# Four seven-product pairs in the V chunk of a hybrid encoder layer, and the sums of x spread over other steps

## The chip, the cores and the metric

The kernel runs on one core of one Trainium2 chip. The metric is the device time of one execution in microseconds (us); of several runs the median is taken. Engines are named as the profile names them: PE (TensorE), DVE (VectorE), ACT (ScalarE), POOL (GpSimd) and SP, whose queue issues the loads.

## What is computed

One layer over 256 tokens of width 4096, all in float32. With its shapes, cut to what matters here:

```python
h = layer_norm(x, emb_ln_g, emb_ln_b)                # 256 x 4096
p = h @ w_in                                         # 4096 -> 13312 columns: conv B, C, h, z; q, k, v; attention gate
y_conv = c_b * centred_short_conv(c_c * c_h, conv_w) * silu(c_z)
y_attn = banded_window_attention(a_q, a_k, a_v, sink) * silu(a_z)
y = concatenate([y_conv, y_attn], -1) @ w_out        # 4096 x 4096
out = layer_norm(DN_ALPHA * h + y, ln_g, ln_b)
```

## The kernel before

**Chunks and pieces.** The columns of `w_in` are worked off in 26 chunks of 512 columns, in the order `IN_ORDER`: K, then V, then four times an attention gate (AZ) and a Q chunk, then the convolution's chunks. A chunk has 32 row tiles of 128 (`kt`). A plain piece holds four of them (128x2048, 1 MB). Each weight piece is split into a high half, which ACT rounds (`split_hi`, L197), and a low half, which DVE gets by a subtraction (`split_lo`, L201). PE then makes three products for each tile of weights: high by high, high by low, low by high (`mm`, L238 to L240). A plain step has 4 x 2 x 3 = 24 matmuls of 512 columns.

**Pairs.** In most chunks some row tiles are worked off two at a time with Strassen's seven products instead of eight (`mm_pair`, L244). A pair is one step of 7 x 3 = 21 matmuls of 256 columns. Its weights come as four blocks of 128x256 (`ws`, 0.5 MB); three more blocks are sums of them, made on DVE by three additions (`sums`, L178 to L180); ACT and DVE then split seven blocks (128x1792). The sums of x that a pair multiplies lie in the tile `SC`. `x_sums` (L609) makes them once for each of six pairs: five additions on DVE into the tile `xs` (L613, L618), then two copies on ACT (L480) and two subtractions on DVE (L481) that write `SC` and one quarter of `xT`. The second half of the even row tile's x in `xT` is overwritten there, so no plain step may use that row tile later. At a chunk's end the partial sums in `pacc` are put together: one copy on ACT (`pair_copy`, L642), four additions on DVE (`pair_sums`, L649 to L652), and two additions of `acc` (`whole`, L657).

**Steps.** A chunk's order is a string: `s` is a plain piece and `S` a pair. Before the change the K and V chunks have eight plain steps each (steps 0 to 7 and 8 to 15), and every chunk from AZ on has `sSsSSsSsSSs`, eleven steps. The first seven steps are written out in the prologue with the first LayerNorm; from step 7 on one loop issues everything, and each engine's queue has the order of this loop:

```python
mm_pair(j) if kind == "pair" else mm(j)
split_hi(j + 3)
for fn, a in later.pop(j, []):
    fn(*a)
...
loads(j)
sums(j + 4)
split_lo(j + 3)
```

So the high half and the low half of step j + 3 are issued at step j, and the sums of a pair one step earlier. `split_hi(j + 3)` writes one of three buffers and so waits for the matmuls of step j. The loads go through four weight buffers in these chunks; a load waits until the step that had the buffer has its low half.

**The chunk ends that matter here.** `end_k` (L487) copies the two accumulators of K to SBUF on ACT at step 7 (L490). `k_turn` (L492), at step 8, transposes them on PE (L476), right behind the matmuls of step 8, and splits the result (L480, L481). `end_v` (L496) splits the two accumulators of V at step 15 directly from PSUM. The mask table `tab` (L458 to L466) is made on DVE just ahead of step 7's work; its first operation waits for POOL.

Of the kernel before, what the change touches and what calls it, by code (L numbers as in the profile page):

```python
# [8 lines left out]
F32 = mybir.dt.float32  # L9
# [5 lines left out]
P = 128  # L15
D = 4096
S = 256
# [17 lines left out]
NPC = KT // PK  # L35
IN_ORDER = [C_K, C_V]
# [4 lines left out]
HW = W // 2  # L41
HT = S // 2
NP = 6
PAIRS = [0, 0] + [NP] * (len(IN_ORDER) - 2)
ORDERS = {0: "s" * 8, NP: "sSsSSsSsSSs"}
OUT = 100
OP = 4
OUT_ORDERS = ["s" * 8] * 2 + ["sSsSsSsSss"] * 4 + ["s" * 8, "", ""]
# [3 lines left out]
def units(ci):  # L52

    q, p, us = 2 * PAIRS[ci] // PK, 0, []
    for u in ORDERS[PAIRS[ci]]:
        if u == "s":
            us.append(("in", ci, q))
            q += 1
        else:
            us.append(("pair", ci, p))  # L60
            p += 1
    assert q == NPC and p == PAIRS[ci]
    return us
# [18 lines left out]
def npairs(ci):  # L82
    return PAIRS[ci] if ci < OUT else OUT_ORDERS[ci - OUT].count("S")

# [10 lines left out]
def encoder_kernel(ctx: ExitStack, tc: tile.TileContext, x, emb_g, emb_b, wi, ws, conv_w, sink, wo, ln_g, ln_b, out):  # L95
# [59 lines left out]
    def loads(j):  # L155

        nonlocal nxt
        while nxt < len(steps) and nxt <= j + 7:
            (u, _), bs = w_bufs(nxt)
            if u > j + (2 if len(bs) > N_W else 3):  # L160
                break
            load(nxt)
            nxt += 1
# [31 lines left out]
    def split_hi(j):  # L195
        wh[j] = half_tile(j, "whi")
        nc.scalar.activation(part(j, wh[j]), part(j, raw[j]), AF.Copy)  # L197

    def split_lo(j):
        wl[j] = half_tile(j, "wlo")  # L200
        nc.vector.tensor_tensor(part(j, wl[j]), part(j, raw[j]), part(j, wh[j]).bitcast(F32), op=ALU.subtract)  # L201
        raw.pop(j)
# [20 lines left out]
    acc = {}  # L223

    def mm(j):
        _, ci, q = steps[j]
        hi, lo = wh.pop(j), wl.pop(j)
        first = j == 0 or steps[j - 1][1] != ci
        last = j == N_IN - 1 or steps[j + 1][1] != ci
        for k in range(PK):  # L230
            kt = q * PK + k
            for i in range(2):
                if first and k == 0:
                    acc[ci, i] = ps_acc.tile([P, W], F32, name="acc")
                a = acc[ci, i]
                xh, xl = xT[:, kt, i * P:(i + 1) * P], xT[:, kt, S + i * P:S + (i + 1) * P]
                hk, lk = hi[:, k * W:(k + 1) * W], lo[:, k * W:(k + 1) * W]
                nc.tensor.matmul(a, xh, hk, start=(first and k == 0), stop=False)  # L238
                nc.tensor.matmul(a, xh, lk, start=False, stop=False)  # L239
                nc.tensor.matmul(a, xl, hk, start=False, stop=(last and k == PK - 1))  # L240
# [3 lines left out]
    def mm_pair(j):  # L244


        _, ci, p = steps[j]
        hi, lo = (t.pop(j).rearrange("p (b w) -> p b w", w=HW) for t in (wh, wl))
        last = p == npairs(ci) - 1
        if p == 0:  # L250
            for k in range(2):
                pacc[ci, k] = ps_p.tile([P, 2, HW], F32, name="pacc")
        a, b = 2 * p, 2 * p + 1
        x = lambda kt, i: (xT[:, kt, i * HT:(i + 1) * HT], xT[:, kt, (2 + i) * HT:(3 + i) * HT])
        sc = lambda n: (SC[:, p, 0, n, :], SC[:, p, 1, n, :])
        p0, p1, c0, c1 = pacc[ci, 0], pacc[ci, 1], acc[ci, 0], acc[ci, 1]
        for (ah, al), w, o, opens, closes in (
                (x(a, 0), 2, p0[:, 0, :], True, False), (x(b, 0), 3, c0[:, 0:HW], False, False),
                (sc(2), 1, c0[:, HW:W], False, False), (x(b, 1), 7, c1[:, 0:HW], False, False),
                (sc(0), 5, p1[:, 1, :], True, False), (x(a, 1) if ci < OUT else sc(3), 6, p0[:, 1, :], False, True),  # L260
                (sc(1), 4, p1[:, 0, :], False, True)):
            nc.tensor.matmul(o, ah, hi[:, w, :], start=(opens and p == 0), stop=False)  # L262
            nc.tensor.matmul(o, ah, lo[:, w, :], start=False, stop=False)  # L263
            nc.tensor.matmul(o, al, hi[:, w, :], start=False, stop=(closes and last))  # L264
# [13 lines left out]
    with tc.tile_pool(name="pro", bufs=1) as pro:  # L278
        warm = small.tile([P, 1], F32, name="sd", bufs=1)
        nc.scalar.activation(warm, eps_t, AF.Abs_reciprocal_sqrt)  # L280
        xs = [pro.tile([P, D], F32, name=f"x{i}") for i in range(2)]
# [171 lines left out]
    pa = ph.enter_context(tc.tile_pool(name="pa", bufs=1))  # L453
# [4 lines left out]
    def build_tab():  # L458
        ti = pa.tile([P, 2, S], F32, name="ti", tag="s")
        nc.gpsimd.iota(ti, pattern=[[-P, 2], [1, S]], base=0, channel_multiplier=-1,  # L460
                       allow_small_or_imprecise_dtypes=True)
        tf = pa.tile([P, 2, S], F32, name="tf", tag="p", bufs=2)
        nc.vector.tensor_scalar(tf, ti, -1.0, None, op0=ALU.mult)
        nc.vector.tensor_tensor(tf, tf, ti, op=ALU.max)
        nc.vector.tensor_scalar(ti, tf, float(WINDOW), NEG, op0=ALU.is_gt, op1=ALU.mult)
        nc.vector.tensor_tensor(tab, ti, tf, op=ALU.subtract)  # L466
# [12 lines left out]
    def halves(hi, lo, src):  # L479
        nc.scalar.activation(hi, src, AF.Copy)  # L480
        nc.vector.tensor_tensor(lo, src, hi.bitcast(F32), op=ALU.subtract)  # L481
# [3 lines left out]
    v = pa.tile([P, 2, 2, W], F32R, name="v")  # L485
# [8 lines left out]
            halves(kT[:, 2 * b:2 * b + 2, 0, :], kT[:, 2 * b:2 * b + 2, 1, :], ps)  # L494

    def end_v(ci, g):  # L496
        for i in range(2):
            halves(v[:, i, 0, :], v[:, i, 1, :], acc.pop((ci, i)))

    def end_z(ci, g):  # L500
        st_["z"] = whole(ci)
# [107 lines left out]
    def x_sums(p, t):  # L609

        x = xT[:, 2 * p:2 * p + 2, :]
        xf = t[:, 0:2 * S].rearrange("p (k t) -> p k t", k=2)
        nc.vector.tensor_tensor(xf, x[:, :, 0:S].bitcast(F32), x[:, :, S:2 * S].bitcast(F32), op=ALU.add)  # L613
        a11, a12, a21, a22 = (xf[:, k, i * HT:(i + 1) * HT] for i in range(2) for k in range(2))
        s = t[:, 2 * S:4 * S].rearrange("p (k t) -> p k t", k=4)
        for k, o0, o1, op in ((0, a21, a22, ALU.subtract), (3, s[:, 0, :], a11, ALU.subtract),
                              (1, a11, a21, ALU.subtract), (2, a12, s[:, 3, :], ALU.add)):
            nc.vector.tensor_tensor(s[:, k, :], o0, o1, op=op)  # L618
        if SC.shape[3] == 4:
            return halves(SC[:, p, 0, :, :], SC[:, p, 1, :, :], s)  # L620
        halves(SC[:, p, 0, :, :], SC[:, p, 1, :, :], s[:, 0:3, :])
        halves(x[:, 0, HT:2 * HT], x[:, 0, 3 * HT:4 * HT], s[:, 3, :])
# [17 lines left out]
    def pair_copy(ci):  # L640
        e = st_["e", ci] = sum_tile(ci)
        nc.scalar.activation(e[:, 0, 0:HW], pacc[ci, 0][:, 0, :], AF.Copy)  # L642
# [11 lines left out]
    def whole(ci):  # L654
        t = st_.pop(("e", ci))
        for i in range(2):
            nc.vector.tensor_tensor(t[:, i, :], acc.pop((ci, i)), t[:, i, :], op=ALU.add)  # L657
        return t
# [60 lines left out]
    def y_lo(q):  # L719
        for hi, lo, y in y_parts(q):  # L720
            nc.vector.tensor_tensor(lo, y, hi.bitcast(F32), op=ALU.subtract)

    build_tab()
    later = {}

    def at(j, fn, *a):
        later.setdefault(j, []).append((fn, a))

    ENDS = [(C_AZ, end_z), (C_V, end_v), (C_K, end_k), (C_Q, end_q), (C_CZ, end_cz), (C_CH, end_ch), (C_CC, end_cc),
            (C_CB, end_cb)]  # L730

# [28 lines left out]
    nxt = n_pro + 6  # L760
    last0 = N_IN - len(ORDERS[PAIRS[-1]])
    for t, f, q in ((3, y_load, 0), (5, y_hi, 0), (6, y_lo, 0), (6, y_load, 1), (7, y_hi, 1), (8, y_lo, 1), (8, y_load, 2),
# [5 lines left out]
    for j in range(n_pro, N_IN):  # L768
        kind, ci, q = steps[j]
        if j == z0 - 18:  # L770
            extra.clear()
        if j == z0 + 6:
            extra.insert(0, (pw, "w6"))
# [4 lines that stand above are left out]
        if kind == "pair" and q == PAIRS[ci] - 1:  # L778
            pair_copy(ci)
            at(j + 1, pair_sums, ci)  # L780
        if ci == 1 and 2 <= q < 2 + NP:
            x_sums(q - 2, pa.tile([P, 4 * S], F32, name="xs", tag="zT"))
        if steps[j + 1][1] != ci or j == N_IN - 1:
            if ci == c_ch0:
                at(j + 4, open_pc)
            if PAIRS[ci]:
                at(j + 1, chunk_end, j + 1, ci)
            else:
                chunk_end(j, ci)
# [3 lines that stand above are left out]
# [176 lines left out]
    for n, (c0, w, pk, j0) in enumerate(chunks):  # L969
        us = out_units(n)  # L970
        np_ = sum(u[0] == "opair" for u in us)
        for t, (kind, _, q) in enumerate(us):
            j = j0 + t
# [117 lines left out]
```

## Time and profile before

| what | value |
|---|---|
| median of 3 runs | 1543.43 us (1542.38 to 1543.45) |
| the profiled execution, its own time | 1543.44 us |
| span of the profile (first to last instruction) | 1541.7 us |
| PE busy | 1525.8 us, 99% of the span |
| DVE busy | 1271.7 us, 82% |
| ACT busy | 756.1 us, 49% |
| granted clock | 1.000 |

All times in the trace count from the span's start. In a timeline a row is: start, duration, engine, line, operation, output and inputs, shape, count, and in brackets the idle time before it and what ended it. A PE row's duration overlaps the next matmul; how long a matmul takes in a row of them is read from the distance between two starts. An engine's duration overlaps a little with the next start too, so what an operation costs a busy queue is the distance from its start to the next one's. In a list of waits a row gives the total, the number of times and the longest.

### The profile page before, as it was taken

The numbers are of one execution on the slowest core, as the hardware profiler recorded it, in microseconds if no ns is written. First come the engines' busy times: TensorE is split into PE (matmuls) and PEld (weight loads), VectorE is DVE, ScalarE is ACT, GpSimd is POOL, SyncE is SP. The second block draws the span as 40 slices with busy tenths as digits, with TensorE's granted clock in tenths as the row PEclk, the third lists the DMA queues.
The fourth block names the chain that finished last, engine by engine and source line by source line (L and its number), as shares of the span: only waits on it lengthen the run. The fifth ranks groups of instructions, "written<-read, shape, count | busy, mean of one in ns | idle before, by whom it ended". The sixth has DMA issues, their size and how long they took to land.

```text
span 1541.7 us, 21128 instructions
## 1 busy us (share of the span) xinstructions
PE 1525.8 (99%) x8654; PEld 1325.1 (86%) x8654; DVE 1271.7 (82%) x1441; ACT 756.1 (49%) x640; POOL 1.3 (0%) x7
## 2 busy tenths in 40 slices
PE   7999999999999999999999999999999999999998
PEld 4888888888888888888888888888888888888897
DVE  7778798888897888898888889888888688888656
ACT  4545556556465554544544445444455444444331
POOL 0000000000000000000000000000000000000000
PEclk9999999999999999999999999999999999999999
DMA  7635554545545456656555655556557756666753
GB/s 283 223 138 203 205 191 169 196 175 182 203 158 188 164 188 238 217 191 208 194 199 191 219 205 186 187 208 218 192 188 274 276 185 225 253 203 235 252 182 140
DMA packets 67392, 313.51 MB, mean 203 GB/s; under 512 B 8064, under 2 KB 12128, under 8 KB 43488
## 3 DMA queue, kind: packets, MB, share of 16 engines
q1 hardware_dynamic: 66288, 310.33, 56.5%
q10 hardware_dynamic: 1008, 1.84, 0.3%
q8 instruction: 68, 1.11, 0.3%
q14 instruction: 28, 0.23, 0.0%
HBM read 304.19 MB, written 7.86 MB: 202 GB/s over the span
## 4 chain that ended last, share of the span: by engine, by line
PE 93%; DVE 3%; issue 2%; ACT 2%; DMA 0%; SPq 0%; ACTq 0%
PE acc L238 15%; PE acc L240 15%; PE acc L239 15%; PE acc L879 7%; PE acc L881 7%; PE acc L880 7%; PE pacc L263 5%; PE pacc L262 5%; PE pacc L264 4%; PE acc L263 3%; PE acc L262 3%; PE acc L264 3%; DVE wlo L201 1%; ACT whi L197 1%; PE att L476 1%
## 5 line engine op out<-in xcount | busy, mean ns | idle before, releaser
L197 ACT ACTIVATE whi<-w 128x2048 fp32r<-128x2048 f32 (+1 forms) x330 | 600.0, 1818 | 671.1 <-PE acc L240 292.3
L201 DVE TENSOR_TENSOR wlo<-w,whi 128x2048 fp32r<-128x2048 f32 (+1 forms) x330 | 712.1, 2164 | 200.1 <-ACT whi L197 198.3
L238 PE MATMUL acc<-whi,xT 128*128 128x512 f32 x1072 | 424.5, 396 | 0.0
L240 PE MATMUL acc<-whi,xT 128*128 128x512 f32 x1072 | 420.1, 392 | 0.0
L239 PE MATMUL acc<-wlo,xT 128*128 128x512 f32 x1072 | 417.4, 389 | 0.7 <-DVE wlo L201 0.7
L240 PEld LDWEIGHTS acc<-whi,xT 128*128 128x128 f32 x1072 | 201.3, 188 | 47.0
L239 PEld LDWEIGHTS acc<-wlo,xT 128*128 128x128 f32 x1072 | 201.3, 188 | 41.6 <-DVE wlo L201 1.0
L238 PEld LDWEIGHTS acc<-whi,xT 128*128 128x128 f32 x1072 | 201.5, 188 | 37.5
L879 PE MATMUL acc<-whi,xT 128*128 128x512 f32 (+1 forms) x496 | 182.9, 369 | 0.0
L881 PE MATMUL acc<-whi,xT 128*128 128x512 f32 (+1 forms) x496 | 181.8, 366 | 0.0
L880 PE MATMUL acc<-wlo,xT 128*128 128x512 f32 (+1 forms) x496 | 180.5, 364 | 0.0
L178 DVE TENSOR_TENSOR w<-w 128x512 f32<-128x512 f32 x154 | 105.2, 683 | 4.5 <-DMA w<-in_ws 4.5
L881 PEld LDWEIGHTS acc<-whi,xT 128*128 128x128 f32 x496 | 93.0, 188 | 16.9
L880 PEld LDWEIGHTS acc<-wlo,xT 128*128 128x128 f32 x496 | 93.1, 188 | 15.5
L879 PEld LDWEIGHTS acc<-whi,xT 128*128 128x128 f32 x496 | 93.2, 188 | 14.2 <-issue 0.4
L263 PE MATMUL acc<-wlo,xT 128*128 128x256 f32 x320 | 89.4, 279 | 0.0
L262 PE MATMUL acc<-whi,xT 128*128 128x256 f32 x320 | 89.3, 279 | 0.0
L264 PE MATMUL acc<-whi,xT 128*128 128x256 f32 x320 | 89.1, 279 | 0.0
L262 PE MATMUL pacc<-whi,xT 128*128 128x256 f32 x304 | 86.9, 286 | 0.0
L263 PE MATMUL pacc<-wlo,xT 128*128 128x256 f32 x304 | 84.9, 279 | 0.0
L264 PE MATMUL pacc<-whi,xT 128*128 128x256 f32 x304 | 84.7, 279 | 0.0
L263 PE MATMUL pacc<-wlo,SC 128*128 128x256 f32 x288 | 81.0, 281 | 0.0
(230 smaller groups left out, 1873.8 us busy)
## 6 DMA issues: line engine op xcount, KB each, us to landing
w<-in_wi SPq DMA_DIRECT2D x134, 1024.0 KB
w<-in_ws SPq DMA_DIRECT2D x154, 512.0 KB
w<-in_wo SPq DMA_DIRECT2D x43, 1024.0 KB
R<-in_wo SPq DMA_DIRECT2D x13, 1024.0 KB
x<-in_x SPq DMA_DIRECT2D x7, 512.0 KB
yl<-yd SPq DMA_DIRECT2D x7, 512.0 KB
xc<-in_x SPq DMA_DIRECT2D x14, 256.0 KB
R<-in_ws SPq DMA_DIRECT2D x6, 512.0 KB
```

What stands on the lines that cost most here:

```text
L178: nc.vector.tensor_tensor(s01, b22, b12.to_broadcast([P, 2, HW]), op=ALU.add)
L197: nc.scalar.activation(part(j, wh[j]), part(j, raw[j]), AF.Copy)
L201: nc.vector.tensor_tensor(part(j, wl[j]), part(j, raw[j]), part(j, wh[j]).bitcast(F32), op=ALU.subtract)
L238: nc.tensor.matmul(a, xh, hk, start=(first and k == 0), stop=False)
L239: nc.tensor.matmul(a, xh, lk, start=False, stop=False)
L240: nc.tensor.matmul(a, xl, hk, start=False, stop=(last and k == PK - 1))
L262: nc.tensor.matmul(o, ah, hi[:, w, :], start=(opens and p == 0), stop=False)
L263: nc.tensor.matmul(o, ah, lo[:, w, :], start=False, stop=False)
L264: nc.tensor.matmul(o, al, hi[:, w, :], start=False, stop=(closes and last))
L879: nc.tensor.matmul(o, yh, hk, start=first, stop=False)
L880: nc.tensor.matmul(o, yh, lk, start=False, stop=False)
L881: nc.tensor.matmul(o, yl, hk, start=False, stop=last)
```

## The change

The V chunk gets four pairs. Its order is `sssSSsSsSs`: six plain steps and four pairs, steps 8 to 17, instead of eight plain steps. All later chunks keep their order and stand two steps later in the count. Since V now has partial sums in `pacc`, its end is the one that pair chunks have, one step late: `pair_copy` at step 16, `pair_sums` at 17, and at 18 `end_v`, which first calls `whole` and then splits the sum from SBUF.

`x_sums`, before at steps 10 to 15, is now called at the steps in `X_SUMS`: 7, 8, 10, 12, 14 and 16. Pairs 0 to 3 are first used at steps 11, 12, 14 and 16, and pairs 4 and 5 in the AZ chunk.

```diff
-PAIRS = [0, 0] + [NP] * (len(IN_ORDER) - 2)
-ORDERS = {0: "s" * 8, NP: "sSsSSsSsSSs"}
+VP = 4
+PAIRS = [0, VP] + [NP] * (len(IN_ORDER) - 2)
+ORDERS = {0: "s" * 8, VP: "sssSSsSsSs", NP: "sSsSSsSsSSs"}
...
     def end_v(ci, g):
+        t = whole(ci)
         for i in range(2):
-            halves(v[:, i, 0, :], v[:, i, 1, :], acc.pop((ci, i)))
+            halves(v[:, i, 0, :], v[:, i, 1, :], t[:, i, :])
...
+    X_SUMS = [NPC + k for k in (-1, 0, 2, 4, 6, 8)]
...
-        if ci == 1 and 2 <= q < 2 + NP:
-            x_sums(q - 2, pa.tile([P, 4 * S], F32, name="xs", tag="zT"))
+        if j in X_SUMS:
+            x_sums(X_SUMS.index(j), pa.tile([P, 4 * S], F32, name="xs", tag="zT"))
```

In the listings below, numbers behind `w` tell weight pieces apart: `w_462` is step 10, `w_492` step 11, `w_500` step 12, and step 13 is `w_561` before and `w_571` after.

DVE at steps 7 to 9, from the mask table on, in the kernel before:

```order
L466 TENSOR_TENSOR tab<-ti,tf 128x512
L201 TENSOR_TENSOR wlo<-w_462,whi 128x2048
L481 TENSOR_TENSOR kT<-att,kT 128x2x256 x2
L201 TENSOR_TENSOR wlo<-w_492,whi 128x2048
L201 TENSOR_TENSOR wlo<-w_500,whi 128x2048
```

The same place on DVE in the changed kernel:

```order
L467 TENSOR_TENSOR tab<-ti,tf 128x512
L615 TENSOR_TENSOR xs<-xT 128x512
L620 TENSOR_TENSOR xs<-xs 128x128 x4
L482 TENSOR_TENSOR SC<-xs,SC 128x384
L482 TENSOR_TENSOR xT<-xs,xT 128x128
L179 TENSOR_TENSOR w_492<-w_492 128x512
L180 TENSOR_TENSOR w_492<-w_492 128x256
L181 TENSOR_TENSOR w_492<-w_492 128x256
L202 TENSOR_TENSOR wlo<-w_462,whi 128x2048
L482 TENSOR_TENSOR kT<-att,kT 128x2x256 x2
```

The first sums of x and the three sums of step 11's weights now stand between the mask table and the low half of step 10.

ACT at steps 7 and 8 in the kernel before, from the high half of step 10 on:

```order
L197 ACTIVATE whi<-w_462 128x2048
L490 ACTIVATE k<-acc 128x512 x2
L197 ACTIVATE whi<-w_492 128x2048
L480 ACTIVATE kT<-att 128x2x256 x2
L197 ACTIVATE whi<-w_500 128x2048
```

The same place on ACT in the changed kernel:

```order
L198 ACTIVATE whi<-w_462 128x2048
L481 ACTIVATE SC<-xs 128x384
L481 ACTIVATE xT<-xs 128x128
L491 ACTIVATE k<-acc 128x512 x2
L198 ACTIVATE whi<-w_492 128x1792
L481 ACTIVATE kT<-att 128x2x256 x2
```

The two copies of the K accumulators, which the transposes on PE read, now stand behind the two copies of the first sums of x.

DVE from the low half of step 12 to that of step 13 in the kernel before:

```order
L201 TENSOR_TENSOR wlo<-w_500,whi 128x2048
L613 TENSOR_TENSOR xs<-xT 128x512
L618 TENSOR_TENSOR xs<-xs 128x128 x4
L481 TENSOR_TENSOR SC<-xs,SC 128x384
L481 TENSOR_TENSOR xT<-xs,xT 128x128
L201 TENSOR_TENSOR wlo<-w_561,whi 128x2048
```

The same stretch in the changed kernel, where step 12 is a pair and `w_630` is the pair of step 14:

```order
L202 TENSOR_TENSOR wlo<-w_500,whi 128x1792
L615 TENSOR_TENSOR xs<-xT 128x512
L620 TENSOR_TENSOR xs<-xs 128x128 x4
L482 TENSOR_TENSOR SC<-xs,SC 128x384
L482 TENSOR_TENSOR xT<-xs,xT 128x128
L179 TENSOR_TENSOR w_630<-w_630 128x512
L180 TENSOR_TENSOR w_630<-w_630 128x256
L181 TENSOR_TENSOR w_630<-w_630 128x256
L202 TENSOR_TENSOR wlo<-w_571,whi 128x2048
```

Three additions for step 14's weights have come in ahead of the low half of step 13.

## Prediction

> **What bounds the kernel now.** I read the page first, then PE's list of waits, then the timelines of PE, DVE and ACT around the V chunk.
>
> ```profile
> PE 1525.8 (99%) x8654; PEld 1325.1 (86%) x8654; DVE 1271.7 (82%) x1441; ACT 756.1 (49%) x640; POOL 1.3 (0%) x7
> PE acc L239 <- DVE wlo L201: 0.7, 1, 0.7
> 143.00:200.00 57.00, 57.00 (x336) 50.39 (x335) 44.50 (x45) 29.56 (x21) 0.00 (x0) 1.00 0.55 193
> ```
>
> PE has no idle time in the AZ and Q stretch from 143 to 200 us (57.00 of 57), and behind the prologue it waits for DVE once: 0.7 us. So PE's own work sets the time, and each us that PE is made to wait anywhere is a us more. That one wait lies right behind the V chunk, in the third step of AZ (step 18).
>
> ```profile
> 118.31 0.28 PE L262 MATMUL pacc<-whi,xT 128*128 128x256 f32 x1
> ...
> 120.79 0.40 PE L238 MATMUL acc<-whi,xT 128*128 128x512 f32 x1
> 121.87 0.51 PE L239 MATMUL acc<-wlo,xT 128*128 128x512 f32 x1 [0.69 <-DVE wlo L201]
> 122.22 0.40 PE L240 MATMUL acc<-whi,xT 128*128 128x512 f32 x1
> ...
> 132.22 0.40 PE L238 MATMUL acc<-whi,xT 128*128 128x512 f32 x1
> 132.45 0.40 PE L239 MATMUL acc<-wlo,xT 128*128 128x512 f32 x1
> ...
> 137.72 0.28 PE L262 MATMUL pacc<-whi,xT 128*128 128x256 f32 x1
> ```
>
> A pair takes 120.79 - 118.31 = 2.48 us, a plain step 137.72 - 132.22 = 5.50 us, one matmul of 512 columns 0.23 us. The wait costs 121.87 - 120.79 - 0.23 = 0.85 us, and the next matmul comes 0.35 instead of 0.23 us later: 0.97 in all. DVE was late there, so the question is what DVE has to do from the end of the prologue on.
>
> ```profile
> 71.26 0.69 DVE L466 TENSOR_TENSOR tab<-ti,tf 128x512 f32<-128x512 f32 x1
> 71.87 2.28 DVE L201 TENSOR_TENSOR wlo<-w,whi 128x2048 fp32r<-128x2048 f32 x1
> 76.16 1.29 DVE L481 TENSOR_TENSOR kT<-att,kT 128x512 fp32r<-128x512 f32 x2 [2.00 <-ACT kT L480]
> 77.36 2.28 DVE L201 TENSOR_TENSOR wlo<-w,whi 128x2048 fp32r<-128x2048 f32 x1
> 82.06 2.29 DVE L201 TENSOR_TENSOR wlo<-w,whi 128x2048 fp32r<-128x2048 f32 x1 [2.41 <-ACT whi L197]
> ...
> 111.85 2.02 DVE L201 TENSOR_TENSOR wlo<-w,whi 128x1792 fp32r<-128x1792 f32 x1
> 113.79 0.68 DVE L613 TENSOR_TENSOR xs<-xT 128x512 f32<-128x512 f32 x1
> 114.51 1.02 DVE L618 TENSOR_TENSOR xs<-xs 128x128 f32<-128x128 f32 x4
> 116.12 0.56 DVE L481 TENSOR_TENSOR SC<-xs,SC 128x384 fp32r<-128x384 f32 x1 [0.59 <-ACT SC L480]
> 116.60 0.28 DVE L481 TENSOR_TENSOR xT<-xs,xT 128x128 fp32r<-128x128 f32 x1
> 116.81 1.29 DVE L481 TENSOR_TENSOR v<-acc,v 128x512 fp32r<-128x512 f32 x2
> 118.01 0.68 DVE L178 TENSOR_TENSOR w<-w 128x512 f32<-128x512 f32 x1
> ...
> 119.53 2.29 DVE L201 TENSOR_TENSOR wlo<-w,whi 128x2048 fp32r<-128x2048 f32 x1
> 121.73 0.68 DVE L178 TENSOR_TENSOR w<-w 128x512 f32<-128x512 f32 x1
> ```
>
> From start to next start DVE pays: a plain low half 2.20 us (119.53 to 121.73), a pair's low half 1.94 (111.85 to 113.79), one `x_sums` 3.02 (113.79 to 116.81, with 0.59 of waiting for ACT inside), the sums of a pair's weights 1.52 (118.01 to 119.53), the halves of kT and of v 1.20 each (76.16 to 77.36, 116.81 to 118.01). For the end of a pair chunk there are rows at the end of AZ:
>
> ```profile
> 155.77 0.41 DVE L649 TENSOR_TENSOR z<-z,pacc 128x256 f32<-128x256 f32 x1
> ...
> 157.54 0.68 DVE L178 TENSOR_TENSOR w<-w 128x512 f32<-128x512 f32 x1
> ...
> 161.26 1.28 DVE L657 TENSOR_TENSOR z<-acc,z 128x512 f32<-128x512 f32 x2
> 162.46 0.68 DVE L178 TENSOR_TENSOR w<-w 128x512 f32<-128x512 f32 x1
> ```
>
> So `pair_sums` costs 1.77 and `whole` 1.20.
>
> **The change, part by part.** *PE's work.* Two plain steps go and four pairs come: 4 x 2.48 - 2 x 5.50 = -1.08 us. With the old wait of 0.97 gone too, the most that the change can win is 2.05 us.
>
> *DVE's work.* Added are four weight sums (6.08), four pair low halves for two plain ones (7.76 - 4.40 = 3.36), `pair_sums` (1.77) and `whole` (1.20): 12.41 us more, in a stretch of which DVE was already late at the end. The six `x_sums` stay as many, but start at step 7 and not at step 10, and that uses the two idle times of 2.00 and 2.41 us in the rows above. That is all the slack there was ahead of them.
>
> *The chain on DVE.* From 71.87, where the mask table is done, I add up what the queue now holds in order, up to the low half of the plain step that is the sixth of AZ (step 23 now, 21 before): six `x_sums` 18.12; sums for the pairs of steps 11, 12, 14, 16, 19, 21, 22 and 24, 8 x 1.52 = 12.16; plain low halves of 10, 13, 15, 17, 18, 20 and 23, 6 x 2.20 + 2.29 = 15.49; pair low halves of 11, 12, 14, 16, 19, 21 and 22, 7 x 1.94 = 13.58; kT 1.20, `pair_sums` 1.77, `whole` 1.20, v 1.20; waits for ACT inside kT and v 0.33, worked out from ACT's order. Sum 65.05: DVE is done at 136.92. Before, PE's second matmul of this step, which reads that low half, ran at 132.45 without waiting. Now it can run at 136.92 + 0.04 (a low half that ended at 119.53 + 2.30 let PE go at 121.87), and the 0.12 of a matmul behind a wait come on top: 137.08 - 132.45 = 4.63 us later.
>
> *The same from PE's side.* I put down for every step when DVE has its low half and when PE gets there. The first wait is not for DVE but for ACT:
>
> ```profile
> 68.19 1.92 ACT L197 ACTIVATE whi<-w 128x2048 fp32r<-128x2048 f32 x1 [3.58 <-PE acc L240]
> 70.01 1.06 ACT L490 ACTIVATE k<-acc 128x512 f32<-128x512 f32 x2
> ...
> 115.56 0.53 ACT L480 ACTIVATE SC<-xs 128x384 fp32r<-128x384 f32 x1 [0.57 <-DVE xs L618]
> 116.00 0.29 ACT L480 ACTIVATE xT<-xs 128x128 fp32r<-128x128 f32 x1
> 116.20 1.06 ACT L480 ACTIVATE v<-acc 128x512 fp32r<-128x512 f32 x2
> 73.48 1.03 PE L476 MATMUL att<-ident,k 128*128 128x128 f32 x8
> ```
>
> The copies of K were ready at 71.07, the transposes began at 73.48. Now the copies stand behind the first `x_sums`: its additions on DVE take 71.87 to 73.61 (1.74 by the rows at 113.79 and 114.51), ACT's two copies for it another 0.64 (115.56 to 116.20), and the K copies 74.28 to 75.34. PE waits there about 1.8 us. Then the low halves of steps 10, 11 and 12 are ready at 78.7, 86.6 and 88.6, ahead of PE (81.8, 87.1, 89.6). That of step 13 has two low halves of pairs, an `x_sums` and the sums of step 14 before it and is ready at 95.3, when PE wants it at 92.2: 3.1 us. After that PE waits 0.7 at step 15, 0.4 at 21 and 0.6 at 23. Together 6.7 of waiting, less 1.08 and 0.97: +4.7, which agrees with the chain. From step 24 on DVE has its halves ahead again (138.8 for a want at 142.4), so nothing is given back later and nothing more is lost.
>
> *Loads.* Each load waits for a low half, so they come later with DVE. The tightest is step 15's: it goes out at 86.6, and ACT wants it at 94.9, 8.3 us later. A load of the same size, issued among others, held ACT until 4.86 us after it was issued:
>
> ```profile
> 1320.71 0.38 SPq L153 DMA_DIRECT2D R<-in_wo  x1
> 1325.57 1.92 ACT L197 ACTIVATE whi<-R 128x2048 fp32r<-128x2048 f32 x1 [1.00 <-DMA R<-in_wo]
> ```
>
> So I cost the loads at nothing; they would have to take 3.4 us longer to be seen.
>
> The sum stands against the profiled execution's 1543.44 us, which is the median (1543.43): 1543.44 + 4.63 = 1548.1 us.
>
> **The rivals.** A measurement of this kernel tells about 0.2%, 3.1 us, from no change.
>
> *The look-ahead hides DVE (faster, 1541.4).* Low halves are issued three steps ahead, and of 99% busy time PE had lost 0.7 us to DVE. If the 12.4 us hid too, 2.05 us would be won: 1541.4. It decides whether the chain from 71.87 is over 4.6 us shorter than I add up, that is, whether DVE had more idle time than the 4.41 us shown. I find none: between 84 and 122 us its only idle times are the waits inside `x_sums`, which I count. Chance 0.05.
>
> *A part of it hides (1546.3).* `x_sums` without its wait for ACT would make the chain 6 x 0.59 = 3.5 us shorter, and half of that gives 1546.3, all of it 1544.6. But DVE's order has nothing else to do between those rows, and the wait was there six times of six:
>
> ```profile
> DVE SC L481 <- ACT SC L480: 5.8, 6, 1.9
> ```
>
> Chance 0.10 for 1544.6 to 1547.0.
>
> *PE runs slower behind the long wait (1548.5 to 1550.2).* The first matmuls of the trace come after 9.2 us without any:
>
> ```profile
> 9.20 3.48 PE L378 MATMUL att<-x,ident 128*128 128x512 f32 x4 [9.20 <-DMA x<-in_x]
> 14.03 5.42 PE L365 MATMUL acc<-first,hT 128*128 128x512 f32 x12
> 9.00:14.00 5.00, 4.59 (x12) 2.01 (x12) 4.69 (x14) 0.77 (x3) 0.00 (x0) 1.00 1.00 413
> ```
>
> They took 0.87 us each, the same shape later 0.45: half speed at first, though the granted clock reads 1.00 in that stretch (the first of the last three numbers), so that this column doesn't show it. If the wait at step 13 (no matmul for 2.95 us, as the first one of the step still runs 0.40) did this again for four such matmuls, PE would lose 4 x 0.42 = 1.7 us. The later waits of 0.7, 0.4 and 0.6 take nearly all of that up, since DVE's chain hardly changes: about +0.4, 1548.5. Twice as long a slow stretch would cost 3.4, of which 2.1 are seen: 1550.2. [...] Chance 0.15.
>
> *The K copies are the only loss (1543.2).* If DVE kept up and only ACT's order cost, 1.80 - 2.05 would leave 1543.2, no change. The same chain speaks against it: with that wait gone PE would come to step 13 earlier and wait there so much longer. Chance 0.05.
>
> **How the numbers follow.** My forecast has the other 0.65. Its own range is 1547.0 to 1549.2: 0.5 us for the rounding of some 40 distances, and a wait that I missed or counted too much (0.6, the size of the small ones). The range for 8 in 10 takes in the slow-clock case and the upper part of the half-hidden one: 1546.0 to 1550.6. Slower by over 0.2% (above 1546.5): 0.65, 0.15 and a little of the half-hidden case, 0.83. Within 0.2%: 0.13. Faster: 0.04.
>
> **What would show it.** Right: PE's list of waits has one of about 1.8 us for ACT at the transposes of K, one of about 3 us for DVE at a plain step some 20 us later, and three under 1 us, and the one of 0.69 is gone; DVE's timeline has no idle time but for ACT from 72 to 101 us; the sixth step of AZ begins its low products near 137 us; from there both traces run alike. Wrong: no wait of over 1 us behind the K chunk, or DVE idle there; then the look-ahead did hide it. Matmuls 0.4 us apart behind the wait would show the slow clock, and a wait of ACT or DVE for a load between 80 and 130 us would show that the loads were not free.

## The result, and the profile after

The changed kernel takes 1548.74 us (median of 6 runs, 1547.95 to 1549.38), the kernel before in the same session 1543.34 (6 runs, 1542.26 to 1543.8): ratio 1.0036, 95% interval 1.0023 to 1.0049. It is slower by 5.4 us; 4.7 were forecast (1548.1 against 1543.43). The profiled execution took 1549.04 us, its span is 1547.0. (Among the experiments below, one execution, the profiled one of `v_sums_left_out`, ran at half pace from end to end, 3084.66 us at a granted clock of 1.00 in the profile; its trace is not compared, and without it the median of that kernel is 1546.97 instead of 1547.02.)

The page's row of busy times:

```profile
PE 1525.5 (99%) x8690; PEld 1324.9 (86%) x8690; DVE 1283.7 (83%) x1461; ACT 759.6 (49%) x643; POOL 1.3 (0%) x7
```

From PE's list of waits (total, times, longest), the rows of the V and AZ chunks, and a last one from the end of the kernel:

```profile
PE acc L240 <- DVE wlo L202: 3.4, 3, 2.7
PE att L477 <- ACT k L491: 1.4, 2, 1.3
PE acc L883 <- DVE w L202: 1.3, 1, 1.3
PE pacc L264 <- DVE wlo L202: 0.3, 1, 0.3
```

DVE has 12.0 us more work (1283.7 for 1271.7; 12.41 were added up), PE 0.3 less (1.08 less was added up; part of the difference is that a matmul just before a wait counts with its whole 0.40 us, and one in a row with 0.23). PE's share is 99% as before: 5 us of waiting don't show in it. They show in the list, as one longest wait of 2.7 for DVE, one of 1.3 for ACT, and small ones. The timeline of PE says where:

```profile
74.60 0.33 PE L477 MATMUL att<-ident,k 128*128 128x128 f32 x1 [1.25 <-ACT k L491]
...
75.83 0.48 PE L239 MATMUL acc<-whi,xT 128*128 128x512 f32 x1
...
87.11 0.28 PE L263 MATMUL pacc<-whi,xT 128*128 128x256 f32 x1
...
92.06 0.40 PE L239 MATMUL acc<-whi,xT 128*128 128x512 f32 x1
95.11 0.50 PE L240 MATMUL acc<-wlo,xT 128*128 128x512 f32 x1 [2.66 <-DVE wlo L202]
...
136.87 0.51 PE L240 MATMUL acc<-wlo,xT 128*128 128x512 f32 x1 [0.34 <-DVE wlo L202]
```

The first row is the first transpose of K, 75.83 the plain step behind them; 92.06 and 95.11 lie in step 13 (plain), 136.87 in step 23, the sixth of AZ. The old wait of 0.69 is gone. On DVE's side, from the first sums of x on:

```profile
71.56 0.68 DVE L615 TENSOR_TENSOR xs<-xT 128x512 f32<-128x512 f32 x1
...
73.89 0.56 DVE L482 TENSOR_TENSOR SC<-xs,SC 128x384 fp32r<-128x384 f32 x1 [0.59 <-ACT SC L481]
...
78.56 1.29 DVE L482 TENSOR_TENSOR kT<-att,kT 128x512 fp32r<-128x512 f32 x2 [0.19 <-ACT kT L481]
...
92.78 4.22 DVE L202 TENSOR_TENSOR wlo<-w,whi 128x2048 fp32r<-128x2048 f32 x2
...
134.53 4.22 DVE L202 TENSOR_TENSOR wlo<-w,whi 128x2048 fp32r<-128x2048 f32 x2
```

Up to 102 us DVE has no idle time but 0.59 in each `x_sums` and 0.19 before kT. The first of the two low halves at 92.78 is that of step 13: it ends about 95.07, and PE goes on at 95.11. The busy time of each engine in two stretches (start and end, length, then PE, PEld, DVE, ACT, POOL with the number of instructions in brackets, then clock, DMA share and GB/s), of the changed kernel:

```profile
74.00:118.00 44.00, 40.18 (x216) 34.18 (x217) 40.16 (x64) 22.48 (x26) 0.00 (x0) 1.00 0.44 156
143.00:200.00 57.00, 57.00 (x345) 50.72 (x344) 43.97 (x45) 30.56 (x21) 0.00 (x0) 1.00 0.57 201
```

and of the kernel before the first of them:

```profile
74.00:118.00 44.00, 44.00 (x196) 36.18 (x195) 33.35 (x57) 20.70 (x24) 0.00 (x0) 1.00 0.44 156
```

In the V chunk PE went from full to 40.18 of 44 us, DVE from 33.35 to 40.16. From 143 us on PE is full again, as before.

Two rows make a ruler for what follows: the last split of LayerNorm's output on DVE, which the change doesn't touch, and the first silu of the convolution on ACT, far behind AZ. Of the kernel before:

```profile
67.57 1.23 DVE L371 TENSOR_TENSOR xT<-hT,xT 128x1024 fp32r<-128x1024 f32 x1
632.73 1.06 ACT L691 ACTIVATE tm<-tm 128x1024 f32<-128x1024 f32 x1
```

and of the changed kernel:

```profile
67.26 1.22 DVE L372 TENSOR_TENSOR xT<-hT,xT 128x1024 fp32r<-128x1024 f32 x1
636.94 1.06 ACT L693 ACTIVATE tm<-tm 128x1024 f32<-128x1024 f32 x1
```

From the one to the other 565.16 us pass before and 569.68 after: **+4.52**. I call this distance the stretch; it leaves out how early the prologue was done and how the last chunks went. It is read from one profiled execution of each kernel, while the times are medians of several.

### The profile page after: what moved, and what is told of

Its sections match the earlier page's. It is cut to its first block, busy times and chain, and to the rows that moved or that the text cites. A ratio compares the mean times of both kernels' runs of the same rounds, so it can differ in the third digit from the quotient of the medians.

```text
span 1547.0 us, 21234 instructions
## 1 busy us (share of the span) xinstructions
PE 1525.5 (99%) x8690; PEld 1324.9 (86%) x8690; DVE 1283.7 (83%) x1461; ACT 759.6 (49%) x643; POOL 1.3 (0%) x7
## 3 DMA queue, kind: packets, MB, share of 16 engines
q10 hardware_dynamic: 1008, 1.84, 0.3%
## 4 chain that ended last, share of the span: by engine, by line
PE 86%; DVE 7%; ACT 3%; DMA 2%; issue 2%; SPq 0%; POOLq 0%; ACTq 0%; DVEq 0%
PE acc L239 14%; PE acc L241 14%; PE acc L240 14%; PE acc L882 6%; PE acc L884 6%; PE acc L883 6%; PE pacc L264 4%; PE pacc L263 4%; PE pacc L265 4%; DVE wlo L202 3%; PE acc L264 3%; PE acc L263 3%; PE acc L265 3%; ACT whi L198 2%; DMA x<-in_x 1%
## 5 line engine op out<-in xcount | busy, mean ns | idle before, releaser
L239 PE MATMUL acc<-whi,xT 128*128 128x512 f32 x1056 | 418.1, 396 | 0.0
L240 PE MATMUL acc<-wlo,xT 128*128 128x512 f32 x1056 | 411.8, 390 | 3.4 <-DVE wlo L202 3.4
L241 PE MATMUL acc<-whi,xT 128*128 128x512 f32 x1056 | 413.7, 392 | 0.0
L883 PE MATMUL acc<-wlo,xT 128*128 128x512 f32 (+1 forms) x496 | 180.6, 364 | 0.2 <-DVE wlo L202 0.2
L883 PEld LDWEIGHTS acc<-wlo,xT 128*128 128x128 f32 x496 | 93.1, 188 | 16.1 <-DVE wlo L202 0.5
L263 PE MATMUL acc<-whi,xT 128*128 128x256 f32 x328 | 91.5, 279 | 0.0
L265 PE MATMUL acc<-whi,xT 128*128 128x256 f32 x328 | 91.4, 279 | 0.0
L263 PE MATMUL pacc<-whi,xT 128*128 128x256 f32 x312 | 89.2, 286 | 0.0
L265 PE MATMUL pacc<-whi,xT 128*128 128x256 f32 x312 | 86.9, 279 | 0.0
```

What stands on the lines that cost most here:

```text
L883: nc.tensor.matmul(o, yh, lk, start=False, stop=False)
```

## The experiments

Theory A is the prediction's: the loss is set by DVE's queue, from the end of the prologue to the sixth AZ step, and the single waits of PE only say where that queue is met. The rival (B) differs from run to run, and each expectation names it: that the order on ACT, the early place of `x_sums`, or the way in which PE runs costs the time by itself. All numbers in one table; "stretch" is against the 565.16 of before, the time against the runs of before in the same session (1543.34 for the change; then 1542.86 up to `sums_only`, 1542.93 up to `v_sums_left_out` and 1543.17 for the next two; 1543.51, a single run, for the last two).

| kernel | time, us | ratio to before, 95% interval | time more | stretch more |
|---|---|---|---|---|
| the change | 1548.74 | 1.0036 (1.0023 to 1.0049) | 5.40 | 4.52 |
| `k_first` | 1549.68 | 1.0042 (1.0029 to 1.0054) | 6.82 | 6.01 |
| `table_late` | 1545.41 | 1.0016 (1.0007 to 1.0025) | 2.55 | 1.71 |
| `reordered` | 1543.14 | 1.0003 (0.9995 to 1.0012) | 0.28 | -0.74 |
| `sums_only` | 1550.91 | 1.0054 (1.004 to 1.0067) | 8.05 | 7.80 |
| `sums_alone` | 1543.40 | 1.0003 (0.9993 to 1.0012) | 0.47 | 0.45 |
| `sums_10_15` | 1552.66 | 1.0062 (1.0047 to 1.0077) | 9.73 | 8.88 |
| `table_twice` | 1551.79 | 1.0057 (1.004 to 1.0074) | 8.86 | 8.55 |
| `v_sums_left_out` | 1547.02 | 1.0025 (1.0016 to 1.0035) | 4.09 | not compared |
| `v_sums_loaded` | 1544.86 | 1.0009 (0.9999 to 1.0018) | 1.69 | 0.77 |
| `v_sums_zeros_again` | 1545.45, one run | | | 2.46 |
| `change_again_1` | 1549.28, one run | | | 4.53 |
| `change_again_2` | 1548.19, one run | | | 4.70 |

### The K copies ahead of the first sums of x

```diff
-        if j in X_SUMS:
+        if j in X_SUMS and j != NPC - 1:
...
+        if j == NPC - 1:
+            x_sums(X_SUMS.index(j), pa.tile([P, 4 * S], F32, name="xs", tag="zT"))
```

The second place is behind `chunk_end`, so `end_k`'s copies come first on ACT.

> Edit: at step 7 the K copies and the end of the K chunk come before the first x_sums, on ACT and DVE. Nothing else moves. Theory A (DVE's queue from the mask table to the low half of step 23 sets the loss, whichever wait shows it): the wait of 1.4 us at the K transposes goes, but PE then comes earlier to steps 11 and 13 and waits there as much longer (about 1.3 at step 11, 3.6 at step 13); the low products of step 23 begin as before near 136.9, and the time stays at that of the changed kernel, 1548.7 (within 0.5). Theory B (each wait is a loss of its own, so ACT's order at the K chunk's end costs its 1.4 us): 1547.3.

Measured 1549.68, no gain. From PE's list of waits, from its timeline, and a stretch of it with the clock (the first of the last three numbers):

```profile
PE acc L240 <- DVE wlo L202: 3.7, 2, 3.4
PE pacc L264 <- DVE wlo L202: 1.0, 1, 1.0
```

```profile
94.70 0.80 PE L240 MATMUL acc<-wlo,xT 128*128 128x512 f32 x1 [3.39 <-DVE wlo L202]
95.29 0.63 PE L241 MATMUL acc<-whi,xT 128*128 128x512 f32 x1
95.72 0.63 PE L239 MATMUL acc<-whi,xT 128*128 128x512 f32 x1
```

```profile
93.60:100.20 6.60, 5.50 (x13) 4.36 (x14) 5.93 (x10) 3.23 (x4) 0.00 (x0) 0.50 0.66 246
```

The wait for ACT at the transposes is gone, and PE waits that much longer for DVE: 1.0 at step 11 and 3.39 at step 13. Step 13's low product starts at 94.70 instead of 95.11, and of these 0.41 us the prologue, which ended 0.40 earlier in this execution (66.86 for 67.26), accounts for all. So the K copies cost nothing of their own. And the third rival shows itself: the clock is at 0.50 and 13 matmuls are 0.43 us apart instead of 0.23. That costs 13 x 0.20 = 2.6 us at this place, of which 1.5 are seen in the stretch (6.01 for 4.52). The prediction had 0.4 seen of 1.7 and 2.1 of 3.4; 2.6 lies between, at 1.3. The way is another, though. The prediction had DVE's chain hardly change; here ACT has to wait with the high half of step 16 for the matmuls of step 13, whose buffer it writes, and DVE waits for that high half:

```profile
102.91 1.70 ACT L198 ACTIVATE whi<-w 128x1792 fp32r<-128x1792 f32 x1 [3.92 <-PE acc L241]
104.64 2.03 DVE L202 TENSOR_TENSOR wlo<-w,whi 128x1792 fp32r<-128x1792 f32 x1 [1.33 <-ACT whi L198]
```

These 1.33 us, which the changed kernel's DVE doesn't have, are nearly all of the 1.5.

### The mask table later

```diff
-    build_tab()
...
+        if j == 28:
+            build_tab()
```

> Edit: the changed kernel with the mask table made at step 28 instead of ahead of step 7; the same instructions, four of DVE and one of POOL moved by some 60 us. Theory A: DVE's chain begins at 68.4 instead of 71.6, so 3.0 us are won: 1545.7; no wait at the K transposes, about 2.0 at step 13, the small waits at 15, 21 and 23 stay. Theory B: only the K wait goes, 1.4 us: 1547.3.

Measured 1545.41. The 2.3 us of the table leave the head of DVE's queue, and with them the 0.81 that its first operation waits for POOL; 2.81 of these 3.1 us are won in the stretch (1.71 for 4.52). No wait for ACT is left at the transposes, and step 13 waits less:

```profile
92.00 0.50 PE L240 MATMUL acc<-wlo,xT 128*128 128x512 f32 x1 [1.80 <-DVE wlo L202]
```

An operation that belongs neither to the V chunk nor to the pairs is worth more than half of the loss, because it stands in the same queue ahead of them.

### The same instructions in another order

```diff
-    X_SUMS = [NPC + k for k in (-1, 0, 2, 4, 6, 8)]
-    build_tab()
+    X_SUMS = [NPC + k for k in (-1, 0, 3, 6, 15, 17)]
...
+        if j == 28:
+            build_tab()
```

`x_sums` at steps 7, 8, 11, 14, 23 and 25: the last two later, for the pairs that only AZ uses.

> Edit: the changed kernel with the mask table at step 28 and x_sums at steps 7, 8, 11, 14, 23 and 25: the same instructions as the changed kernel, only later. Theory A: DVE has each low half in time, waits of 0.5 and 0.2 us are left in AZ, and the time is 6.0 us below the changed kernel, 1542.7, some 1 us below the kernel before. Theory B: the wait at step 13, behind two pairs in a row, stays with its 2.7 us: 1547.3 at best.

Measured 1543.14, not to be told from before. All that is left of PE's waits for DVE in this kernel:

```profile
PE acc L240 <- DVE wlo L202: 0.7, 2, 0.4
```

With the same instructions the 4.52 of the stretch go to -0.74. So the loss is no cost of the pairs as such, nor of the instructions that were added; it is their place in DVE's queue. It also shows how little there was to win: 2.05 at most by the prediction, and 0.74 with most waits gone.

### The sums of x spread, without pairs in V

The first try, `sums_only`, had no V pairs (`VP = 0`) and the steps of the changed kernel:

> Edit: no pairs in V (eight plain steps, its end from PSUM as before), only x_sums at steps 7, 8, 10, 12, 14 and 16. Theory A: PE waits about 1.8 us (by the trace of the changed kernel 1.4) at the K transposes and 0.5 and 0.6 us at two steps of AZ, since the first x_sums stand before other work and the last two stand where DVE is already full; 2.2 us slower than before, 1545.5. Theory C (the pairs of V alone are the loss, the spread itself costs nothing or wins the old wait of 0.97): 1542.4 to 1543.4.

It took 1550.91, but not for the reason that was asked. The first sums of x, at step 7, overwrite a part of row tile 0, which V's first plain piece at step 8 still reads. So this kernel makes V's products for that row tile from the overwritten part, and PE waits until it is written:

```profile
73.85 0.80 PE L239 MATMUL acc<-whi,xT 128*128 128x512 f32 x1 [5.57 <-ACT xT L481]
```

My mistake: without pairs the first places allowed are 8, 8 and 9. The second try keeps to them:

```diff
-VP = 4
+VP = 0
...
-    X_SUMS = [NPC + k for k in (-1, 0, 2, 4, 6, 8)]
+    X_SUMS = [NPC + k for k in (0, 1, 2, 4, 6, 8)]
```

> The V chunk in plain products as before (no V pairs, no sums of their weights, no pair_sums or whole), with the x_sums spread over steps 8, 9, 10, 12, 14 and 16 as far as the row tiles that V still reads allow. Theory A: DVE has no more work than before, only in another order; two waits of 0.5 and 0.6 us at AZ's third and fifth step take the place of the one of 0.7: +0.4 at most, 1543.4 to 1543.9. Theory B (the spread costs by itself): most of the 5.4 us, 1547 or more.

Measured 1543.40, +0.45 in the stretch, as theory A has it. Spreading the sums of x costs nothing that these runs could tell; nor does it win, as before lost under 1 us. (The first place, step 7, can't be tried without pairs.)

### The V pairs with the sums of x where they were

```diff
-    X_SUMS = [NPC + k for k in (-1, 0, 2, 4, 6, 8)]
+    X_SUMS = [NPC + k for k in (2, 3, 4, 5, 6, 7)]
```

> The four V pairs as in the changed kernel, but the six x_sums back where they were before, behind steps 10 to 15. Theory A (DVE's queue up to the sixth AZ step sets the loss): the two idle times of DVE behind the prologue are no longer filled, so the queue is done later: about 8.1 us above before at that step and 3.2 above the changed kernel, 1551.4 us; PE waits about 2.7 us at step 11, 4.2 at step 12, 1.1 and 1.2 at steps 17 and 18, and matmuls 0.43 us apart may follow the longest wait. Theory B (the early x_sums is what costs, by standing ahead of K's copies and low halves): at or under the changed kernel's 1548.7.

Measured 1552.66, stretch +8.88 where 8.1 was expected. The size is nearly right; the place of the waits only in part. At steps 11 and 12 PE does not wait for the low half but, a little later in the step, for the sums of x themselves, which are made just one step ahead:

```profile
87.59 0.38 PE L263 MATMUL acc<-whi,SC 128*128 128x256 f32 x1 [1.75 <-ACT SC L481]
...
94.32 0.39 PE L263 MATMUL acc<-whi,SC 128*128 128x256 f32 x1 [2.19 <-ACT SC L481]
```

Behind both waits the clock is at 0.50 for 3.4 us (from 87.98 and from 94.80, by windows of 0.2 us). The windows around the first:

```profile
84.60:87.90 3.30, 1.54 (x11) 1.25 (x9) 0.86 (x4) 2.52 (x3) 0.00 (x0) 1.00 0.45 153
88.00:91.30 3.30, 3.20 (x15) 3.12 (x15) 3.23 (x6) 0.00 (x0) 0.00 (x0) 0.50 0.02 5
```

The early `x_sums` of the change thus win 4.4 us against this; the spreading is what keeps its loss at 5.

### The mask table twice

```diff
     build_tab()
+    build_tab()
```

> The changed kernel with the mask table made twice ahead of the V chunk: 2.26 us more on DVE behind the prologue, before the first x_sums. Theory A: all of it is seen behind AZ, +2.3, 1551.0 us. The wait for the K copies grows to about 4 us and matmuls 0.43 us apart may follow it; that slow stretch is taken up by the later waits for DVE. Theory B (DVE's slack hides what is added ahead of step 10): 1548.7.

Measured 1551.79, and 4.03 in the stretch against the changed kernel (8.55 less 4.52), where 2.3 were expected. DVE's idle times say where the rest comes from:

```profile
72.35 0.43 DVE L464 TENSOR_SCALAR tf<-ti 128x512 f32<-128x512 f32 x1 [0.67 <-POOL ti L461]
94.17 0.56 DVE L482 TENSOR_TENSOR SC<-xs,SC 128x384 fp32r<-128x384 f32 x1 [1.16 <-ACT SC L481]
107.66 2.03 DVE L202 TENSOR_TENSOR wlo<-w,whi 128x1792 fp32r<-128x1792 f32 x1 [0.34 <-ACT whi L198]
```

The second table waits 0.67 for POOL, so the first `x_sums` starts 3.0 later, counted from the ruler's first row. Then 1.16 instead of 0.59 and 0.34 instead of nothing are lost, where DVE waits for ACT and ACT for matmuls. 3.0 + 0.57 + 0.34 = 3.9 of the 4.03. Those last two come from slow matmuls, behind PE's two waits:

```profile
77.64 0.33 PE L477 MATMUL att<-ident,k 128*128 128x128 f32 x1 [4.26 <-ACT k L491]
...
98.70 0.61 PE L240 MATMUL acc<-wlo,xT 128*128 128x512 f32 x1 [1.82 <-DVE wlo L202]
```

```profile
71.70:75.00 3.30, 1.68 (x8) 1.04 (x6) 2.54 (x5) 0.00 (x0) 0.56 (x1) 1.00 0.38 146
75.10:78.40 3.30, 0.60 (x3) 0.41 (x4) 2.61 (x9) 1.70 (x4) 0.00 (x0) 1.00 0.00 0
78.50:81.80 3.30, 3.30 (x12) 2.81 (x11) 3.08 (x4) 2.41 (x3) 0.00 (x0) 0.50 0.00 0
...
95.60:98.90 3.30, 1.48 (x11) 1.16 (x11) 3.27 (x4) 2.28 (x2) 0.00 (x0) 1.00 0.02 6
99.00:102.30 3.30, 3.30 (x9) 2.50 (x9) 3.17 (x6) 1.14 (x2) 0.00 (x0) 0.50 0.73 256
```

Here, as in `k_first`, the slow clock lengthens DVE's chain itself, which I had said it hardly does: DVE is then waiting for PE by way of ACT.

### The weight sums of the V pairs left out

```diff
+        if steps[j][1] == 1:
+            nc.gpsimd.memset(r1 if len(raw[j].shape) == 3 else t[:, 4:8, :], 0.0)
+            return
```

> The changed kernel without the DVE additions that make the weight sums of the four V pairs (GpSimd writes zeros in their place, so V comes out wrong); all else as in the changed kernel. It takes four times 1.52 us off DVE's queue, all of it ahead of step 21. Theory A: the longest wait, at step 13, shrinks by as much as stood before it, and the mark behind AZ comes 4.1 us earlier than in the changed kernel: 1544.6 us. Theory B (the order on ACT and PE, not the amount of DVE's work): 1548 or more.

Measured 1547.02, 2.4 more than theory A allows and 1.0 less than B's least. Neither held, so it was profiled once more, and beside it a version in which POOL writes nothing:

> The same kernel as v_sums_left_out once more, for a profile at full pace. Its time was 1547.0, where DVE's shorter queue alone gives 1544.6. If GpSimd's writing of zeros holds DVE up (in the profile at half pace a 128x512 DVE operation beside such a write took 2.03 us, and 0.43 elsewhere), the mask table and up to two other operations of DVE are 1 to 1.6 us longer here, and the first x_sums starts about 1.6 us later than in the changed kernel. If not, DVE's rows are as in the changed kernel and the 2.4 us lie elsewhere.

```diff
+        elif is_pair(j) and a == 1:
+            nc.sync.dma_start(out=to, in_=wi[0])
...
-        if j >= len(steps) or not is_pair(j):
+        if j >= len(steps) or not is_pair(j) or steps[j][1] == 1:
```

> The changed kernel without the DVE additions that make the weight sums of the four V pairs, and with nothing written in their place by GpSimd: those four steps load a full 128x2048 tile (1 MB, not 0.5 MB) of other weights, so V is not the reference's. Theory A (DVE's queue): 6.08 us come off DVE ahead of step 21, of which about 1.3 are lost in a longer wait for the copies of kT; the wait of 2.7 at step 13 and those behind it go, the one of 1.4 at the transposes of K stays, and the mark behind AZ comes 4.1 to 4.6 us earlier than in the changed kernel: about 1544.4 us. Theory B (the order on ACT and PE, not the amount of DVE's work): a time near the 1547.0 of the version whose zeros GpSimd writes, or above.

With the zeros, on POOL, DVE and PE:

```profile
69.16 1.84 POOL L180 MEMSET w<- 128x1024 f32 x2
69.25 2.03 DVE L467 TENSOR_SCALAR tf<-ti 128x512 f32<-128x512 f32 x1 [0.81 <-POOL ti L464]
76.14 0.33 PE L480 MATMUL att<-ident,k 128*128 128x128 f32 x1 [2.85 <-ACT k L494]
```

With the loads instead:

```profile
69.25 0.43 DVE L466 TENSOR_SCALAR tf<-ti 128x512 f32<-128x512 f32 x1 [0.81 <-POOL ti L463]
...
89.46 0.56 DVE L484 TENSOR_TENSOR SC<-xs,SC 128x384 fp32r<-128x384 f32 x1 [2.44 <-ACT SC L483]
74.54 0.33 PE L479 MATMUL att<-ident,k 128*128 128x128 f32 x1 [1.25 <-ACT k L493]
```

One DVE operation beside POOL's writes took 1.60 us longer, the wait at the transposes is 1.60 longer (2.85 for 1.25), and the stretch 1.69 (2.46 for 0.77). Without that, 1544.86 was measured for 1544.4, and the stretch is 3.75 shorter than that of the change, for 4.1 to 4.6 expected. So the 6.08 us of weight sums are worth 3.75. Of the rest, DVE idles 1.85 in one `x_sums` (2.44 for 0.59), and not at the copies of kT, where the expectation had it: with less work it comes to a point where it waits for ACT, and ACT for PE. The amount of DVE's work decides, as long as there is no slack. What was my experiment's own cost (POOL in DVE's way) is thus taken out of it. One thing is not shown: the execution traced with the zeros took 1545.45, 1.6 less than the median of that kernel, so its trace needn't hold all that made the others slow.

### The changed kernel twice more

For the slow clock, which the change's own profile didn't show, the changed kernel was profiled again, two times.

> The changed kernel once more, for a second profile. In three experiments PE's granted clock fell to 0.50 for 3.4 us, or twice that, after windows of 3.4 us in which PE was idle for 51% or more, and not after one with 49%. If such windows run free of the kernel, PE's wait of 2.66 us at step 13 escapes only where a window ends in the middle 0.7 us of it; in about 3 of 4 executions the clock falls to 0.50 behind it, matmuls are 0.43 us apart for 3.4 us, and the execution is 0.4 to 1.3 us longer. [...]

> As change_again_1, a third profile of the same kernel: by free windows the clock falls to 0.50 behind step 13's wait in about 3 of 4 executions, and where it falls the window of 3.4 us that ends there has PE idle for half of it or more; by the length of the wait alone it stays at 1.00.

They took 1549.28 and 1548.19 us. Step 13's low product, and what followed, in the first:

```profile
94.74 0.50 PE L240 MATMUL acc<-wlo,xT 128*128 128x512 f32 x1 [2.85 <-DVE wlo L202]
```

```profile
95.00:98.40 3.40, 3.40 (x16) 2.78 (x16) 3.21 (x6) 1.25 (x2) 0.00 (x0) 1.00 0.70 258
```

and in the second:

```profile
94.61 0.80 PE L240 MATMUL acc<-wlo,xT 128*128 128x512 f32 x1 [2.87 <-DVE wlo L202]
```

```profile
90.80:94.10 3.30, 0.93 (x7) 0.61 (x6) 3.23 (x5) 1.58 (x1) 0.00 (x0) 1.00 0.25 101
94.30:97.60 3.30, 2.99 (x7) 2.42 (x8) 3.23 (x5) 1.72 (x1) 0.00 (x0) 0.50 0.51 196
```

The same kernel with the same wait (2.85 and 2.87): the clock stays at 1.00 in one execution and falls to 0.50 for 3.4 us in the other. So the length of the wait alone doesn't decide it. That windows run free of the kernel is not shown by this: one profile of three with a fall, for three of four expected, is too few to weigh. It cost nearly nothing: the stretch is 4.53 above before in the first and 4.70 in the second. The later waits for DVE took the slow stretch up, as the prediction's third rival has it: of the three small ones only the last, of 0.32 us, is left.

## Why the prediction was right

**The chain on DVE: right.** From the first `x_sums` (71.56) to PE's low product of step 23 (136.87) pass 65.31 us; the sum of 65.05 with 0.04 and 0.12 gives 65.21. Against before (132.45, with the chain's start at 71.87) that is 4.42 later, or 4.73 from the same start; 4.63 was forecast. Five kernels that are made to change the length or the order of this queue (`table_late`, `reordered`, `table_twice`, `v_sums_loaded` and `v_sums_zeros_again`) moved the stretch with it. Where PE still waits for the low half of step 23, its low product there, counted from the ruler's first row, can be set beside the stretch: against before it came 4.73 us later in the change, 1.81 in `table_late`, 8.70 in `table_twice`, 0.96 in `v_sums_loaded` and 2.67 in `v_sums_zeros_again`, and the stretch grew by 4.52, 1.71, 8.55, 0.77 and 2.46. So the loss is complete at that step, as the prediction had it.

**The waits on PE: right in kind and place, each a little smaller.** At the transposes 1.4 are listed, not 1.8: the first of them needs the first copy only and began at 74.60. But the loss is as forecast. In the kernel before the plain step behind them started here:

```profile
74.27 0.48 PE L238 MATMUL acc<-whi,xT 128*128 128x512 f32 x1
```

It is 75.83 now, 1.56 later, or 1.87 from the same chain start. At step 13 it is 2.66, not 3.1: counted from the chain's start PE arrived some 0.4 later, mostly since the 48 matmuls from 75.83 to 87.11 were 0.235 us apart, not 0.23. With DVE's end fixed, a later arrival is only a shorter wait. Three waits of 0.3 to 0.4 follow (in the list: 3.4 in all less 2.7, and 0.3) where 0.7, 0.4 and 0.6 were forecast. (The five waits of the prediction, as printed, add up to 6.6, not 6.7; the sum of 4.63 comes from the chain and doesn't hang on it.)

**Nothing is given back, nothing more is lost behind AZ: right to the end of the stretch.** In both kernels PE is busy 57.00 of 57 us from 143 on. The loads, costed at nothing, held neither ACT nor DVE anywhere between 78 and 145 us. (In the two further profiles DVE was idle for 0.53 and 0.43 us up to 138.9, behind the chain's end, and PE did not wait for it; what ended that was not shown.)

**The rivals.** The look-ahead hid nothing: DVE had no idle time that I had not counted. Six waits of 0.59 inside `x_sums` were there again. That the K copies are the only loss is refuted by `k_first`. The slow clock set in behind step 13's wait in one of three profiles of the changed kernel and cost 0.2 there, under the 0.4 that the rival had. In `k_first`, with a wait of 3.39, it cost 1.5, by way of DVE's chain.

**What stays open.** The median rose by 5.40, the stretch by 4.52. The difference of 0.9 lies outside the stretch, and the prediction's sum had nothing for it. By the table it is 0.8 to 1.0 in six of the seven kernels with V pairs that have both numbers, and 0.3 in `table_twice`; without V pairs it is 0.0 and 0.25. About 0.3 of it lies outside the span too: the time less the span is 2.0 to 2.1 us in all six runs of the changed kernel and 1.7 to 1.9 in those of before. For the two profiled executions the parts add up: 4.52 in the stretch, 0.31 less in the prologue, 1.09 more behind the stretch and 0.30 outside the span make the 5.60 between 1549.04 and 1543.44. What lies behind the stretch is not explained. In the changed kernel PE waits 1.3 us near the end for the last output weights (the row for L883 above), which it didn't before; but that can't be all of it, since `reordered`, with a difference of 1.0, has no such row, nor has `change_again_1`, in which this part is even longer (910.6 us for 910.1 in the change, 909.5 in `change_again_2` and 909.0 before). One to three profiles don't settle it.

## What to carry to other kernels

Where a helper engine feeds the bounding one, add up its whole queue from the last point at which it was ahead to the next, in order, and compare the end: the single waits only tell where the difference is met, and removing one (`k_first`) moves it to the next. An edit that adds work to such a queue can be paid for by moving other work out of the stretch (the mask table, the two `x_sums` that are used later), and that is the first thing to try when the added instructions themselves are right. Before that, see how much there is to win: here 2 us at most for 12 us of DVE's work.

## What the runs showed of the hardware

**Waits of nearly the same length: the clock fell with some and not with others.** PE's granted clock went to 0.50 in or behind waits of 5.57 us (`sums_only`), 4.26 and 1.82 (`table_twice`), 3.39 (`k_first`), 2.87 (`change_again_2`), 2.19 and 1.75 (`sums_10_15`), and stayed at 1.00 behind 2.85 (`change_again_1` and `v_sums_zeros_again`), 2.66 (the change) and the 1.80 of `table_late`. In `table_twice`, by windows of 0.2 us, it falls at 78.45 and 98.95 and comes back at 81.9 and 102.35: each fall lasts 3.4 us, and the two are 20.5 apart. The falls in `sums_10_15` and `change_again_2` last 3.4 us too, those in `k_first` and `sums_only` 6.8. Nor does the share of PE's busy time just before tell it in these rows. The window from 95.60 to 98.90 of `table_twice` has PE busy for 1.48 of 3.30 us (45%), that from 84.60 to 87.90 in `sums_10_15` for 1.54 (47%), and the clock fell behind both. Behind 71.70 to 75.00 in `table_twice`, with 1.68 (51%), it did not, and neither behind 91.50 to 94.70 in `change_again_1`, with 0.39 of 3.20 (12%). What decides was not shown.

**The column of the clock is an average.** Over the span it reads 0.997 in `sums_10_15` and 0.998 in `k_first`, `table_twice` and `change_again_2`; only a window of a few us shows the 0.50. The prediction took from the first matmuls (0.87 us apart at 1.00) that the column doesn't show a slow clock. Within an execution it does (0.50 in `k_first`, with matmuls 0.43 us apart); at the start it read 1.00 all the same.

**An operation of DVE took longer beside writes of POOL, another did not.** One 128x512 operation of DVE took 2.03 us instead of 0.43 while POOL wrote two 128x1024 tiles (1.84 us from 69.16 in `v_sums_zeros_again`), and ended 0.28 us after them. DVE's subtraction for kT, at 78.68 beside another such write (0.95 us from 78.51), took its usual 1.29. Why the one was held up and the other not was not shown.
